# Batched matmul: the stores of batches 25 and 26 queued behind the last load instead of between the loads of batches 29 to 31

## The chip, the core and the metric

The kernel runs on one core of one Trainium2 chip. The metric is device microseconds (us) of one execution. Most executions of one kernel agree within 0.3%; a change counts as faster or slower from 2% on, with a 95% interval. A ratio of two kernels is the mean time of the fast runs of one over the mean of the fast runs of the other in the same rounds, so it isn't quite the ratio of the medians quoted beside it. A run is called fast if it isn't over 1.5% above the fastest one of its kernel.

Names used throughout: x29 is the load of x for batch 29, w29 that of its weight, s25 the store of batch 25's result. The last three batches' stores are named by half where they are issued by half (s31 first half, s31 second half). The "software queue" is the DMA queue that GpSimd (POOL) issues to; it carries all loads but the first x, and they are turned from float32 into bfloat16 on the way. The "hardware queue" is the one that SyncE (SP) issues to. Both run on the same 16 DMA engines.

## The reference

```python
batch, m, k, n = 32, 512, 1024, 768
x      = randn(batch, m, k)   # float32
weight = randn(batch, k, n)   # float32
out    = np.matmul(x, weight) # float32, 32 x 512 x 768
```

The kernel has to read 167.8 MB (67.1 of x, 100.7 of weights) and write 50.3 MB. Nothing is used twice, so no traffic can be saved.

## The kernel before

Each batch loads x and its weight as bfloat16, transposes x on the tensor engine, multiplies into PSUM (the tensor engine's result memory), copies the result to SBUF, the on-chip memory ("evacuation" below), and stores it. This is the part that the change touches (cuts are marked with `# ...`):

```python
CHUNKED = {B - 4: (4, 4), B - 3: (4, 4), B - 2: (4, 4), B - 1: (4, 2, 2)}
AHEAD = 3
LATE = 4
# ... pools: w has 4 buffers, x 5, out 7

def load_x(b):
    xs[b] = x_pool.tile([P, MT, K], BF16, name="x_sb")
    nc.gpsimd.dma_start(out=xs[b], in_=x_view[b])

def load_w(b):
    ws[b] = w_pool.tile([P, KT, N], BF16, name="w_sb")
    at = 0
    for n in CHUNKED.get(b, (KT,)):     # the last weights come in two or three pieces
        nc.gpsimd.dma_start(out=ws[b][:, at:at + n, :], in_=w_view[b, :, at:at + n, :])
        at += n

# ... first loads
for b in range(B):
    if b + AHEAD + 1 < B:
        load_x(b + AHEAD + 1)
    if b + AHEAD < B:
        load_w(b + AHEAD)
    if 0 < b <= B - LATE:               # stores 0 to 27: software queue
        nc.gpsimd.dma_start(out=out_view[b - 1], in_=outs[b - 1])
    if b == B - 1:                      # stores 28 to 30: hardware queue
        halves = [slice(pair * N2, (pair + 1) * N2) for pair in range(2)]
        nc.sync.dma_start(out_view[b - 1, :, halves[0]], outs[b - 1][:, halves[0]])
        for late in range(B - LATE, B - 2):
            nc.sync.dma_start(out_view[late], outs[late])
        nc.sync.dma_start(out_view[b - 1, :, halves[1]], outs[b - 1][:, halves[1]])
    outs[b] = out_pool.tile([P, MT * N], F32, name="out_sb")
    # ... transposes, matmuls, evacuation; batch 31 stores each half on the
    #     hardware queue as soon as it is evacuated
```

The order in the software queue at the end is thus: x29 w28 s24 x30 w29 s25 x31 w30 s26 w31 s27.

Of the kernel before, what the change touches and what calls it, by code (L numbers as in the profile page):

```python
# [12 lines left out]
@with_exitstack  # L13
def kernel(
    ctx: ExitStack,
    tc: tile.TileContext,
    x: bass.AP,
    weight: bass.AP,
    out: bass.AP,
):  # L20
    nc = tc.nc
    B, M, K = x.shape
    _, _, N = weight.shape
    P = 128
    MT = M // P
    KT = K // P
    JT = KT // 2
    N2 = 2 * N
    CHUNKED = {B - 4: (4, 4), B - 3: (4, 4), B - 2: (4, 4), B - 1: (4, 2, 2)}
    AHEAD = 3  # L30
    LATE = 4

    const = ctx.enter_context(tc.tile_pool(name="const", bufs=1))
    first_pool = ctx.enter_context(tc.tile_pool(name="first", bufs=1))
    w_pool = ctx.enter_context(tc.tile_pool(name="w", bufs=4))
    x_pool = ctx.enter_context(tc.tile_pool(name="x", bufs=5))
    xT_pool = ctx.enter_context(tc.tile_pool(name="xT", bufs=8))
    out_pool = ctx.enter_context(tc.tile_pool(name="out", bufs=7))
    tpsum = ctx.enter_context(tc.tile_pool(name="tpsum", bufs=2, space=bass.MemoryType.PSUM))
    mpsum = ctx.enter_context(tc.tile_pool(name="mpsum", bufs=2, space=bass.MemoryType.PSUM))  # L40



    w_view = weight.rearrange("b (ki ko) n -> b ki ko n", ki=P)
    x_view = x.rearrange("b (mi mo) k -> b mi mo k", mi=P)
    out_view = out.rearrange("b (mi mo) n -> b mi (mo n)", mi=P)

    xs, ws, outs = {}, {}, {}

    def banks():  # L50
        return [mpsum.tile([P, 512], F32, name=f"pm{i}") for i in range(3)]
# [8 lines that stand above are left out]
        for n in CHUNKED.get(b, (KT,)):  # L60
            nc.gpsimd.dma_start(out=ws[b][:, at:at + n, :], in_=w_view[b, :, at:at + n, :])  # L61
            at += n

    def transpose(b, mt):

        pt = tpsum.tile([P, JT, P], F32, name="pt")
        pairs = xs[b].bitcast(F32)
        for j in range(JT):
            nc.tensor.transpose(pt[:, j, :], pairs[:, mt, j::JT], ident)  # L69
        xT = xT_pool.tile([P, JT, P, 2], BF16, name="xT")  # L70
        nc.vector.tensor_copy(  # L71
            xT.rearrange("p j m r -> p (j m r)"), pt.bitcast(BF16).rearrange("p j m -> p (j m)")
        )
        return xT

    def transpose_first(mt):

        xT = xT_pool.tile([P, JT, P, 2], BF16, name="xT")
        for h in range(2):
            pt = tpsum.tile([P, JT, P], F32, name="pt")  # L80
            for i in range(JT):
                nc.tensor.transpose(pt[:, i, :], x_first[:, mt, JT * h + i::KT], ident)  # L82
            nc.vector.tensor_copy(  # L83
                xT[:, 2 * h:2 * h + 2].rearrange("p j m r -> p j r m"),
                pt.rearrange("p (j r) m -> p j r m", r=2),
            )
        return xT



    SPLITS = (
        ((0, 0, 0, 512), (1, 0, 512, N - 512)),
        ((1, N - 512, 0, 1024 - N), (2, 0, 1024 - N, N2 - 1024)),
    )

    def matmuls(pm, half, xT, b, kos, together):
        for ko in kos:
            for i, (bank, at, off, size) in enumerate(SPLITS[half]):
                shares = half == 1 and i == 0
                nc.tensor.matmul(  # L100
                    pm[bank][:, at:at + size],
                    xT[:, ko // 2, :, ko % 2],
                    ws[b][:, ko, off:off + size],
                    start=(ko == 0 and not (together and shares)),
                    stop=(ko == KT - 1),
                    skip_group_check=together,
                )

    def evacuate(b, pair, pm):
        o = outs[b][:, pair * N2:(pair + 1) * N2]  # L110
        nc.scalar.copy(o[:, 0:512], pm[0])  # L111
        nc.vector.tensor_copy(o[:, 512:1024], pm[1])  # L112
        nc.scalar.copy(o[:, 1024:N2], pm[2])  # L113

    with tc.manual_schedule():
        x_first = first_pool.tile([P, MT, K], F32)
        nc.sync.dma_start(x_first, x_view[0])
        load_w(0)
        ident = const.tile([P, P], F32)
        make_identity(nc, ident)  # L120
        for b in range(1, AHEAD):
            load_x(b)
            load_w(b)
        load_x(AHEAD)

        for b in range(B):
            if b + AHEAD + 1 < B:
                load_x(b + AHEAD + 1)
            if b + AHEAD < B:
                load_w(b + AHEAD)  # L130
            if 0 < b <= B - LATE:
                nc.gpsimd.dma_start(out=out_view[b - 1], in_=outs[b - 1])  # L132
            if b == B - 1:
                halves = [slice(pair * N2, (pair + 1) * N2) for pair in range(2)]
                nc.sync.dma_start(out_view[b - 1, :, halves[0]], outs[b - 1][:, halves[0]])
# [4 lines that stand above are left out]
            if b not in CHUNKED:  # L140
                turn = transpose if b else lambda _, mt: transpose_first(mt)
                xT = {mt: turn(b, mt) for mt in (0, 1)}
                for pair in range(2):
                    pm = banks()
                    for half in range(2):
                        if pair == 0:
                            matmuls(pm, half, xT[half], b, range(KT), False)
                            xT[2 + half] = turn(b, 2 + half)
                        else:
                            matmuls(pm, half, xT[2 + half], b, range(KT), False)  # L150
                    evacuate(b, pair, pm)
                continue
            xT = {0: transpose(b, 0)}
            pms = [banks() for _ in range(2)]
            at = 0
            for n in CHUNKED[b]:
                last = at + n == KT
                for mt in range(MT):
                    if mt + 1 not in xT and mt + 1 < MT:
                        xT[mt + 1] = transpose(b, mt + 1)  # L160
                    matmuls(pms[mt // 2], mt % 2, xT[mt], b, range(at, at + n), True)
                    if last and mt % 2 == 1:
                        pair = mt // 2
                        evacuate(b, pair, pms[pair])
                        if b == B - 1:
                            nc.sync.dma_start(out_view[b, :, halves[pair]], outs[b][:, halves[pair]])
                at += n
# [30 lines left out]
```

## Time and profile before

| what | value |
|---|---|
| time, median of 3 runs | 517.46 us (517.2 to 518.03) |
| span of the profiled execution | 515.2 us |
| DMA engines busy, 38 of the 40 slices | 90% or more |
| tensor engine busy | 83% |
| HBM traffic over the span | 423 GB/s |

First the page of the profile. The digit rows give the busy share of each of 40 equal slices in tenths (9 is 90% or more). GB/s counts a casting load at its two-byte side, so a slice of pure loads shows about 215 and one of pure stores about 425, for the same load on the engines. The last line is the chain of work that ended last, by engine.

```profile
span 515.2 us, 5979 instructions
...
PE   0999898798788888788887899787998787999793
...
DMA  8999999999999999999999999999999999999996
GB/s 254 219 215 213 218 274 273 254 239 277 276 275 270 234 270 276 273 274 244 253 278 274 275 256 241 275 276 275 266 243 263 275 279 269 247 251 274 274 384 275
...
DMA 88%; PE 8%; issue 1%; POOL 1%; DVE 0%; ACT 0%; POOLq 0%
```

DMA is full almost from end to end, and the chain is 88% DMA. How the queue is paced is seen in GpSimd's timeline of the kernel before: start, duration, line and operation, and in brackets the idle time before and what ended it.

```profile
373.09 0.53 POOL L55 DMA_DIRECT2D x_sb<-in_x_dram  x1 [6.66 <-DMA w_sb<-in_weight_dram]
376.75 0.53 POOL L61 DMA_DIRECT2D w_sb<-in_weight_dram  x1 [3.13 <-DMA out_dram<-out_sb]
381.68 0.54 POOL L132 DMA_DIRECT2D out_dram<-out_sb  x1 [4.40 <-DMA x_sb<-in_x_dram]
388.90 0.53 POOL L55 DMA_DIRECT2D x_sb<-in_x_dram  x1 [6.68 <-DMA w_sb<-in_weight_dram]
```

Each issue waits for an earlier transfer to land: an x issue for a weight, a weight's for a store, a store's for an x. That is the transfer eight places earlier, so about eight are always under way (the page's median from issue to landing is 39.6 to 43.2 us for whole transfers, some eight of them). The gaps are therefore the durations of transfers: 7.2 us for a weight (3.15 MB read), 3.66 for a store (1.57 MB), 4.9 for x (2.1 MB), 15.8 us a batch, at some 430 GB/s. 32 times 15.8 is 506 of the 515.2 us.

The end of the kernel, in two views of the kernel before. First the busy time of each engine in stretches of the end, with the granted clock (the share of its full clock that the tensor engine was given), the mean DMA share of 16 engines and GB/s in the last columns:

```profile
core 0: us, PE busy (x) PEld busy (x) DVE busy (x) ACT busy (x) POOL busy (x), PEclk, DMA share, GB/s
480.00:492.00 12.00, 11.15 (x61) 7.04 (x62) 2.07 (x3) 1.15 (x2) 0.00 (x0) 0.86 1.03 285
492.00:504.00 12.00, 11.70 (x77) 7.85 (x75) 3.36 (x5) 1.19 (x3) 0.00 (x0) 1.00 1.02 413
504.00:508.00 4.00, 2.78 (x17) 1.46 (x15) 1.38 (x2) 2.29 (x4) 0.00 (x0) 1.00 0.82 346
508.00:511.00 3.00, 0.00 (x0) 0.00 (x0) 0.00 (x0) 0.00 (x0) 0.00 (x0) 0.73 0.96 395
511.00:515.00 4.00, 0.00 (x0) 0.00 (x0) 0.00 (x0) 0.00 (x0) 0.00 (x0) 0.50 0.16 66
```

Then three lines of its timelines: the first matmuls of batch 30, the last of batch 31, and the issue of batch 31's two stores.

```profile
480.85 1.55 PE L100 MATMUL pm<-w_sb,xT 128*128 128x512 bf16 x8 [3.38 <-DMA w_sb<-in_weight_dram]
...
498.81 7.96 PE L100 MATMUL pm<-w_sb,xT 128*128 128x512 bf16 x48
...
506.12 1.63 SPq L166 DMA_DIRECT2D out_dram<-out_sb  x2
```

The tensor engine waits 3.38 us for w30 and works almost without a break from then to 506.8 us. DMA share drops to 0.82 just there, between 504 and 508 us; batch 31's stores are issued only from 506.12 us on.

### The profile page before, as it was taken

The numbers are of one execution on the slowest core, as the hardware profiler recorded it, in microseconds if no ns is written. First come the engines' busy times: TensorE is split into PE (matmuls) and PEld (weight loads), VectorE is DVE, ScalarE is ACT, GpSimd is POOL, SyncE is SP. The second block draws the span as 40 slices with busy tenths as digits, with TensorE's granted clock in tenths as the row PEclk, the third lists the DMA queues.
The fourth block names the chain that finished last, engine by engine and source line by source line (L and its number), as shares of the span: only waits on it lengthen the run. The fifth ranks groups of instructions, "written<-read, shape, count | busy, mean of one in ns | idle before, by whom it ended". The sixth has DMA issues, their size and how long they took to land.

```text
span 515.2 us, 5979 instructions
## 1 busy us (share of the span) xinstructions
PE 429.3 (83%) x2576; PEld 279.5 (54%) x2576; DVE 129.8 (25%) x196; ACT 76.2 (15%) x129; POOL 51.7 (10%) x102
## 2 busy tenths in 40 slices
PE   0999898798788888788887899787998787999793
PEld 0666465465455555455554556454665455665461
DVE  0433232313223313133132232222331223232231
ACT  0011111111011111111111111010111111111011
POOL 3010100011001010100101001100101010111000
PEclk9999899989889989799898999898999889899897
DMA  8999999999999999999999999999999999999996
GB/s 254 219 215 213 218 274 273 254 239 277 276 275 270 234 270 276 273 274 244 253 278 274 275 256 241 275 276 275 266 243 263 275 279 269 247 251 274 274 384 275
DMA packets 14857, 135.64 MB, mean 263 GB/s; under 512 B 1648, under 2 KB 1648, under 8 KB 3312
## 3 DMA queue, kind: packets, MB, share of 16 engines
q0 software_dynamic: 13824, 126.88, 96.8%
q1 hardware_dynamic: 1008, 8.39, 4.0%
q8 instruction: 20, 0.33, 0.2%
q14 instruction: 5, 0.04, 0.0%
HBM read 167.77 MB, written 50.33 MB: 423 GB/s over the span
## 4 chain that ended last, share of the span: by engine, by line
DMA 88%; PE 8%; issue 1%; POOL 1%; DVE 0%; ACT 0%; POOLq 0%
DMA w_sb<-in_weight_dram 40%; DMA out_dram<-out_sb 25%; DMA x_sb<-in_x_dram 23%; PE pm L100 7%; PE pt L69 1%; POOL w_sb L61 0%; POOL x_sb L55 0%; DVE out_sb L112 0%; DVE xT L71 0%; ACT out_sb L113 0%; POOL ident masks.py:199 0%; POOL ident masks.py:197 0%; POOLq L132 0%; POOLq L61 0%; POOLq masks.py:199 0%
## 5 line engine op out<-in xcount | busy, mean ns | idle before, releaser
L100 PE MATMUL pm<-w_sb,xT 128*128 128x256 bf16 (+1 forms) x2048 | 374.5, 342 | 65.2 <-DMA w_sb<-in_weight_dram 63.7
L100 PEld LDWEIGHTS <-xT 128*128 128x128 bf16 x2048 | 207.5, 102 | 207.7 <-issue 72.5
L71 DVE COPY xT<-pt 128x1024 bf16<-128x1024 bf16 x124 | 82.8, 689 | 230.0 <-PE pt L69 230.0
L111 ACT COPY out_sb<-pm 128x512 f32<-128x512 f32 x64 | 37.5, 585 | 293.2 <-PE pm L100 293.2
L112 DVE COPY out_sb<-pm 128x512 f32<-128x512 f32 x64 | 43.9, 687 | 128.1 <-PE pm L100 128.1
L69 PEld LDWEIGHTS pt<-ident,x_sb 128*128 128x128 f32 x496 | 72.6, 207 | 6.3 <-issue 1.0
L69 PE MATMUL pt<-ident,x_sb 128*128 128x128 f32 x496 | 75.1, 285 | 0.0
L113 ACT COPY out_sb<-pm 128x512 f32<-128x512 f32 x64 | 37.5, 586 | 137.3 <-PE pm L100 137.2
L55 POOL DMA_DIRECT2D x_sb<-in_x_dram x31 | 16.4, 532 | 176.8 <-DMA w_sb<-in_weight_dram 151.3
L61 POOL DMA_DIRECT2D w_sb<-in_weight_dram x37 | 19.7, 534 | 126.3 <-DMA out_dram<-out_sb 59.7
L132 POOL DMA_DIRECT2D out_dram<-out_sb x28 | 15.0, 537 | 118.1 <-DMA x_sb<-in_x_dram 56.4
L82 PE MATMUL pt<-ident,x_first 128*128 128x128 f32 x32 | 6.0, 351 | 12.3 <-DMA x_first<-in_x_dram 12.3
L82 PEld LDWEIGHTS pt<-ident,x_first 128*128 128x128 f32 x32 | 5.0, 204 | 12.9 <-issue 12.2
L83 DVE CAST xT<-pt 128x512 bf16<-128x512 f32 x8 | 5.6, 726 | 19.4 <-PE pt L82 19.1
L111 ACT ACT_TABLE_LOAD x1 | 1.3, 1283 | 0.7 <-PEq L182 0.7
masks.py:199 POOL TENSOR_SCALAR_AFFINE_SELECT ident<-ident 128x128 f32<-128x128 f32 x1 | 0.3, 287 | 0.1
masks.py:197 POOL MEMSET ident<- 128x128 f32 x1 | 0.2, 223 | 0.0
L182 POOL MEMSET const-float32-0.0<- 128x1 f32 x1 | 0.1, 98 | 0.2 <-issue 0.2
L182 POOL MEMSET const-bfloat16-1.0<- 128x1 bf16 x1 | 0.1, 101 | 0.0
L182 POOL MEMSET const-uint8-127<- 128x1 uint8 x1 | 0.1, 101 | 0.0
L182 POOL MEMSET const-float32-1.0<- 128x1 f32 x1 | 0.1, 98 | 0.0
## 6 DMA issues: line engine op xcount, KB each, us to landing
w_sb<-in_weight_dram POOLq DMA_DIRECT2D x28, 1536.0 KB, 43.2
out_dram<-out_sb POOLq DMA_DIRECT2D x28, 1536.0 KB, 42.0
x_sb<-in_x_dram POOLq DMA_DIRECT2D x31, 1024.0 KB, 39.6
w_sb<-in_weight_dram POOLq DMA_DIRECT2D x7, 768.0 KB, 31.4
out_dram<-out_sb SPq DMA_DIRECT2D x4, 768.0 KB, 7.6
out_dram<-out_sb SPq DMA_DIRECT2D x2, 1536.0 KB, 13.7
x_first<-in_x_dram SPq DMA_DIRECT2D x1, 2048.0 KB, 11.4
w_sb<-in_weight_dram POOLq DMA_DIRECT2D x2, 384.0 KB, 27.5
```

The lines of the kernel that those rows point to most:

```text
L55: nc.gpsimd.dma_start(out=xs[b], in_=x_view[b])
L61: nc.gpsimd.dma_start(out=ws[b][:, at:at + n, :], in_=w_view[b, :, at:at + n, :])
L69: nc.tensor.transpose(pt[:, j, :], pairs[:, mt, j::JT], ident)
L71: nc.vector.tensor_copy(xT.rearrange("p j m r -> p (j m r)"), pt.bitcast(BF16).rearrange("p j m -> p (j m)"))
L82: nc.tensor.transpose(pt[:, i, :], x_first[:, mt, JT * h + i::KT], ident)
L83: nc.vector.tensor_copy(xT[:, 2 * h:2 * h + 2].rearrange("p j m r -> p j r m"), pt.rearrange("p (j r) m -> p j r m", r=2),)
L100: nc.tensor.matmul(pm[bank][:, at:at + size], xT[:, ko // 2, :, ko % 2], ws[b][:, ko, off:off + size], start=(ko == 0 and not (together an ...
L111: nc.scalar.copy(o[:, 0:512], pm[0])
L112: nc.vector.tensor_copy(o[:, 512:1024], pm[1])
L113: nc.scalar.copy(o[:, 1024:N2], pm[2])
L132: nc.gpsimd.dma_start(out=out_view[b - 1], in_=outs[b - 1])
L182: nc = _bacc.Bacc("TRN2", target_bir_lowering=False, num_devices=1)
```

## The change

Its intent: the last loads should not stand behind stores that nobody waits for, so that the tensor engine gets its last operands earlier.

```diff
+    HELD = 3
...
+        pending = []
         for b in range(B):
             if b + AHEAD + 1 < B:
                 load_x(b + AHEAD + 1)
             if b + AHEAD < B:
                 load_w(b + AHEAD)
-            if 0 < b <= B - LATE:
-                nc.gpsimd.dma_start(out=out_view[b - 1], in_=outs[b - 1])
+            if b <= B - LATE:
+                if b > 0:
+                    pending.append(b - 1)
+                if b + AHEAD < B - HELD or b == B - LATE:
+                    for at in pending:
+                        nc.gpsimd.dma_start(out=out_view[at], in_=outs[at])
+                    pending = []
```

The order in the software queue becomes: x29 w28 s24 x30 w29 x31 w30 w31 s25 s26 s27. No transfer, byte or instruction is added or removed.

## The prediction

> **What bounds the kernel now.** The DMA engines, nearly from first microsecond to last. The page's slices show DMA at 9 tenths or more in 38 of 40; the chain that ended last is 88% DMA, 8% PE. In GpSimd's timeline a batch between 341 and 408 us takes 15.8 us, a sum of transfers: 7.2 us for a weight (3.15 MB read), 3.66 for a store (1.57 MB), 4.92 for x (2.1 MB), all near 430 GB/s. 32 times 15.8 is 506 of the span's 515.2 us. PE is 83% busy and waits 63.7 us for weights (view of waits). Each software-queue issue waits for the landing of the one eight before it (x_sb issues release on a weight, weights on a store, stores on an x_sb).
>
> **What the change does.** It adds and removes no transfer, byte or instruction. The queue's end goes from x29 w28 s24 x30 w29 s25 x31 w30 s26 w31 s27 to x29 w28 s24 x30 w29 x31 w30 w31 s25 s26 s27. x31 and w30 are ahead by one store (3.66 us), w31 by two (7.3 us). With seven output buffers no evacuation waits for the held stores. Several transfers stay queued at each issue, so nothing starves.
>
> Before, w30's first half landed at 480.7 us and PE had idled 3.4 us for it; w31 landed 491.7 to 495.4, before PE missed it. After, w30 should land near 477.0, w31 between 484.4 and 488.1. Batch 29 ends near 477.6, so batch 30 follows almost without a gap; batch 31 should end near 503 instead of 507.4.
>
> **How much lies on the critical path: almost none.** What ends the kernel is the drain of stores. DMA share falls to 0.82 in 504 to 508 us (windows), which looks like 0.75 us of waiting for batch 31's stores. But that is a mean of 16 engines. The Trainium skill ("DMA: Bandwidth & Descriptors", section "Why a DMA increments its semaphore by 16 and not by 1") says that each engine posts its own +1. The trace records these increments; for one store they spread over 4.6 us. The slowest engine's, for the last stores, come at 504.60, 508.25, 510.13, 511.95 and 513.79 us: 3.65 us per whole store, 1.82 to 1.88 per half, the full rate, without a hole. Only the fast engines idled. Issuing the last stores 4 us earlier lengthens the slowest one's queue and doesn't shorten its work.
>
> A small cost: two queues carry stores together for longer. Before, store 27 with half a store took 5.54 us (495.41 to 500.95) for 2.36 MB, 426 GB/s against 430: over some 9 MB about 0.2 us. I estimate a gain of 0 to 0.8 us and a cost of 0 to 0.3.
>
> **Predicted: 517.3 us** (before 517.46), range 516.2 to 518.3; faster by over 2%: 0.01, within 2%: 0.98, slower by over 2%: 0.01.
>
> **What would show each step.** Right: w30 lands near 477 and PE's wait for it falls from 3.4 us to under 1; PE's last matmul ends near 503; yet the last store's increment stays within 0.7 us of 513.8. DMA share stays near 1.0 through 508. Wrong: PE's end doesn't move (the stores hadn't delayed the loads), or the last increment comes earlier as PE does (the stores' issue was on the path), or over 1 us later (a long pure-store phase is slower than the mix).
>
> **What would make it wrong.** A different rate when both queues only write; the spread of the engines, which grew from 3.55 to 4.6 us after 420 us and may fall otherwise in another run (about 1 us either way).

## The result, and the profile after

| | before | after |
|---|---|---|
| median | 517.15 us (516.99 to 518.03, 6 runs) | 517.17 us (517.0 to 519.47, 6 runs) |
| ratio of fast runs | | 1.0003, 95% interval 0.9987 to 1.002 |

The same time. The profiled execution of the changed kernel was by chance its longest one (519.47 us, span 517.7; the five others took 517.0 to 517.53). These are lines of its page: the span, DMA, GB/s and the chain by engine.

```profile
span 517.7 us, 5931 instructions
...
DMA  8999999999999999999999999999999999999995
GB/s 254 218 217 213 216 273 274 263 230 275 277 273 276 240 257 276 274 278 257 242 272 275 276 270 241 262 275 271 265 243 251 277 275 263 252 242 214 305 425 245
...
DMA 75%; PE 20%; DVE 1%; issue 1%; another core or an unknown queue 1%; ACT 0%; POOLq 0%
```

Since such a run is no fair partner, the unaltered changed kernel was run and profiled once more (run after_again, below: 516.95 us, span 515.1; a single run, so its state is put down as unknown, but its time lies with the fast runs). The comparison uses that trace. Its windows, with the same columns as before:

```profile
480.00:492.00 12.00, 11.80 (x77) 7.95 (x76) 3.35 (x5) 2.35 (x4) 0.00 (x0) 1.00 1.04 344
492.00:504.00 12.00, 11.42 (x70) 7.22 (x72) 3.27 (x6) 2.00 (x4) 0.00 (x0) 1.00 1.01 425
504.00:508.00 4.00, 0.00 (x0) 0.00 (x0) 0.20 (x1) 0.30 (x1) 0.00 (x0) 0.84 0.99 416
508.00:511.00 3.00, 0.00 (x0) 0.00 (x0) 0.00 (x0) 0.00 (x0) 0.00 (x0) 0.50 0.72 301
511.00:515.00 4.00, 0.00 (x0) 0.00 (x0) 0.00 (x0) 0.00 (x0) 0.00 (x0) 0.50 0.15 61
```

And the same three places of its timelines (the line numbers have moved):

```profile
479.37 1.48 PE L101 MATMUL pm<-w_sb,xT 128*128 128x512 bf16 x8 [0.30 <-DVE xT L72]
...
495.72 7.96 PE L101 MATMUL pm<-w_sb,xT 128*128 128x512 bf16 x47
...
503.03 1.63 SPq L173 DMA_DIRECT2D out_dram<-out_sb  x2
```

All that the change aimed at has happened. The tensor engine no longer waits for w30 (0.30 us for a copy of VectorE in place of 3.38 us for a weight). Its last matmul ends at 503.7 us instead of 506.8, the last stores are issued 3.1 us earlier, and the dip of 504 to 508 us is filled: 0.99 in place of 0.82. Yet the span is 515.1 against 515.2 us. What was gained at 504 to 508 us is missing at 508 to 511, where the share is now 0.72 in place of 0.96.

The reason lies below that mean of 16 engines. Each of this kernel's 103 transfers has sixteen increments of its semaphore in the trace (1,648 in all), one for each engine. For the last transfers these are the times of the first and of the last of the sixteen increments, in us (worked out from the records of the trace, rounded to 0.01):

```
            before               after_again
            first    last        first    last
w29 end     463.91  468.54       463.83  468.51     <- same queue up to here
w30 part 1  476.07  480.71       472.35  477.04
w31 end     490.78  495.41       483.39  488.07
s28         499.98  504.60       499.89  504.59
s29         503.64  508.25       503.55  508.23
s30 half 2  505.47  510.13       505.40  510.08
s31 half 1  509.20  511.95       507.24  511.93
s31 half 2  511.09  513.79       509.09  513.77
```

The loads come 3.7 and 7.3 us earlier, as intended. But the column of the slowest engine ends at the same time. (The records name no engine. That the last increment is each time that of the same engine is read from the lag, which is 4.61 to 4.67 us for each of s28, s29 and s30 half 2 before.) In the kernel before, its increments for s28, s29 and the halves follow each other after 3.65, 1.88, 1.82 and 1.84 us: full speed, no hole. It never waited for batch 31's stores, since it was still busy with the earlier ones. Only the fast engines waited (their increment for s31's second half came at 511.09 us), and only they have gained: 2.0 us. The slowest one has gained 0.02 us, and the kernel ends with it.

### The profile page after: what moved, and what is told of

It is laid out like the page before. It is cut to its first block, busy times and chain, and to the rows that moved or that the text cites. A ratio compares the mean times of both kernels' runs of the same rounds, so it can differ in the third digit from the quotient of the medians.

```text
span 517.7 us, 5931 instructions
## 1 busy us (share of the span) xinstructions
PE 423.7 (82%) x2528; PEld 278.5 (54%) x2576; DVE 129.9 (25%) x196; ACT 76.2 (15%) x129; POOL 51.7 (10%) x102
## 2 busy tenths in 40 slices
DMA packets 14857, 135.64 MB, mean 262 GB/s; under 512 B 1648, under 2 KB 1648, under 8 KB 3312
## 4 chain that ended last, share of the span: by engine, by line
DMA 75%; PE 20%; DVE 1%; issue 1%; another core or an unknown queue 1%; ACT 0%; POOLq 0%
DMA w_sb<-in_weight_dram 32%; DMA out_dram<-out_sb 25%; PE pm L101 17%; DMA x_sb<-in_x_dram 16%; DMA x_first<-in_x_dram 2%; PE pt L70 2%; PE pt L83 1%; DVE xT L72 1%; DVE out_sb L113 1%; ACT out_sb L114 0%; POOLq L138 0%; POOLq L62 0%; POOLq L56 0%
## 5 line engine op out<-in xcount | busy, mean ns | idle before, releaser
L101 PE MATMUL pm<-w_sb,xT 128*128 128x256 bf16 (+1 forms) x2000 | 369.0, 339 | 68.6 <-DMA w_sb<-in_weight_dram 63.0
```

What stands on the lines that cost most here:

```text
L101: nc.tensor.matmul(pm[bank][:, at:at + size], xT[:, ko // 2, :, ko % 2], ws[b][:, ko, off:off + size], start=(ko == 0 and not (together an ...
```

## The experiments

"Idle matmuls" below are 20 or 40 matmuls of 512 columns at the start of batch 31, whose result the real ones overwrite; they lengthen the tensor engine's work without touching a transfer.

```diff
             at = 0
+            if b == B - 1:
+                for _ in range(20):        # or 40
+                    nc.tensor.matmul(pms[0][0][:, 0:512], xT[0][:, 0, :, 0],
+                                     ws[b][:, 0, 0:512], start=True, stop=True, skip_group_check=True)
             for n in CHUNKED[b]:
```

All the differences below are under 2%, so by the rule above each kernel is "the same"; they are read from the ratios and their intervals.

**Theory:** the slowest DMA engine is busy from start to end, so the time is the sum of its transfers; the tensor engine has slack, which the change widens. **Rivals:** the end follows the tensor engine, and a gain there is eaten by a slower phase of pure stores; or the dip in the DMA share is on the path.

### 1 to 4: how much slack the tensor engine has

> The kernel before, with 20 idle matmuls of 512 columns (about 0.23 us each, 4.6 us together, overwritten afterwards, so the result stays right) at the start of batch 31. My theory (the slowest DMA engine is busy to the end; the tensor engine has slack of about 2.7 us before the last store, worked out from the trace: an unhindered last half store lands 3.1 us after its issue plus its predecessor's 0.5, that is at 511.05, and it landed at 513.79): +1.9 us. Rival 1 (the end follows batch 31's last evacuation): +4.6 us. Rival 2 (nothing before the drain matters at all): 0.

> The same 20 idle matmuls in the changed kernel. My theory: the change has moved the tensor engine's end ahead by some 4.5 us and so widened its slack from 2.7 to about 7 us: 0 against the kernel before, within 0.5. Rival 1 (end follows the last evacuation, and the change's gain of 4.5 us there is eaten by a slower store phase): +4.6 us like the other one.

> 40 idle matmuls, 9.2 us, in the kernel before. My theory: +6.5 us (9.2 less the slack of 2.7). Rival 1: +9.2. Rival 2: 0.

> 40 idle matmuls, 9.2 us, in the changed kernel. My theory: +2 us (9.2 less a slack of 7), thus 4.5 us less than the kernel before with the same burden: the reordering does take 4.5 us from the tensor engine's chain, which is worth nothing until that chain is made the longer one. Rival 1: +9.2.

All four ran with 11 runs of the kernel before (median 517.04 us). All results were right.

| idle matmuls | in the kernel before | in the changed kernel |
|---|---|---|
| 20 | 519.5 us, ratio 1.0042 (1.003 to 1.0054) | 517.13 us, ratio 1.0 (0.9988 to 1.0012) |
| 40 | 522.92 us, ratio 1.0106 (1.0092 to 1.0121) | 518.94 us, ratio 1.004 (1.0028 to 1.0052) |

In us (517.1 times the ratio less one): +2.2 and +5.5 before, 0 and +2.1 after. The expected values were +1.9, +6.5, 0 and +2. Rival 1 had foreseen 4.6 and 9.2 in all of them, rival 2 nothing in the kernel before. The issue of batch 31's stores in the four traces (in the order before with 20 and 40, after with 20 and 40):

```profile
511.22 1.63 SPq L172 DMA_DIRECT2D out_dram<-out_sb  x2
```

```profile
517.58 1.63 SPq L172 DMA_DIRECT2D out_dram<-out_sb  x2
```

```profile
506.37 1.63 SPq L179 DMA_DIRECT2D out_dram<-out_sb  x2
```

```profile
510.64 1.63 SPq L179 DMA_DIRECT2D out_dram<-out_sb  x2
```

An estimate from the trace of before: its fast engines finished s31 at 511.09 us with an issue at 506.12, which is 4.97 us for both halves. By that rule the four would end no earlier than 516.19, 522.55, 511.34 and 515.61 us. Their last increments came at 516.35, 522.72, 514.01 and 515.78. The first, second and fourth are set by the late issue, within 0.2 us. The third is set by the slowest engine's other work, 0.2 us from the 513.8 of both plain kernels. So the issue becomes the limit only if it comes later than about 508.8 us (513.8 less 5.0). The kernel before issues at 506.12 and has 2.7 us of slack; the changed one issues at 503.03 in its trace and has 5.8 there.

That 5.8 us is low for the changed kernel. In its trace the granted clock was 0.79 and 0.64 between 464 and 470 us, and batch 30's matmuls began only at 479.37 us. In the traces with 20 and 40 idle matmuls the clock was 1.00 there, and they began at 477.93 and 477.88 us. The 40 idle matmuls delayed the real ones by 9.1 us and cost 2.1, which leaves a slack of about 7 us, as was expected; by the issue times of these two traces it is 7.2 to 7.3.

One size was off: +5.5 us with 40 idle matmuls before, where +6.5 was expected. In the trace of before the tensor engine ran for 4 us (482 to 486) at a granted clock of 0.52 and 0.62; runs without such a stretch would have more slack. That is argued, not shown: the traces with idle matmuls in the old order have such a stretch too (0.56 and 0.59 with 20; 0.50 and 0.74, 2 us later, with 40). The profiled run of this kernel was its longest, 525.85 us, because w30 came 2.3 us late there, so it isn't used for the size.

### 5 and 6: one store taken away

```diff
-            if 0 < b <= B - LATE:
+            if 0 < b <= B - LATE and b - 1 != 25:
```

(in the changed kernel: `if at == 25: continue` in the loop over `pending`)

> The kernel before without the store of batch 25 (result wrong in that batch on purpose). My theory (time is the sum of the transfers on the slowest engine): -3.65 us, one store. Rival (the order of the loads sets the end): about the same here, since loads move ahead too.

> The changed kernel without the store of batch 25, which stands behind all loads there (result wrong in that batch on purpose). My theory: -3.65 us against the kernel before, as much as in the other order. Rival (the loads and the tensor engine behind them set the end): 0, since no load moves.

The results are wrong in batch 25. Measured beside 517.36 us (7 runs): 513.77 us, ratio 0.9927 (0.9907 to 0.9947), in the kernel before, and 513.8 us, ratio 0.9926 (0.9904 to 0.9947), in the changed one. A store's 3.65 us is a ratio of 0.9929. Taking 1.57 MB away is worth its transfer time wherever it stands in the queue; moving it is worth nothing.

### 7: less work for the tensor engine at the end

```diff
         for ko in kos:
+            if b == B - 1 and ko in (4, 5):
+                continue
```

> The kernel before with a quarter of batch 31's matmuls left out (result wrong in that batch on purpose), so the tensor engine ends about 2.7 us earlier and no transfer changes. My theory: 0, within 0.5. Rival (the DMA idle time of 504 to 508 us is on the path): -0.75 us; rival (end follows the last evacuation): -2.7.

The result is wrong in batch 31. 517.2 us beside 517.36, ratio 0.9991 (0.9973 to 1.0009). The stores were issued at 503.61 us instead of 506.12, and the last increment came at 513.94. This does to the tensor engine's end nearly what the change does, without the change, and it is worth as little.

### 8: five stores held back instead of three

```diff
-    HELD = 3
+    HELD = 5
```

> The changed kernel with stores 23 to 27 held back instead of 25 to 27: the loads move ahead by up to two more stores, the pure store phase grows from 7 to 9 stores. My theory: 0, within 0.5, since no byte changes. Rival (a gain from earlier loads and a cost of a longer pure store phase cancel in the change): they need not cancel twice, so some -0.5 or +0.5 us or more.

Right result, 517.4 us beside 517.36, ratio 0.9994 (0.9976 to 1.0012). Batch 31's stores were issued at 500.57 us, 5.5 us earlier than in the kernel before; the last increment came at 514.21. So the phase of pure stores can be made longer still without gain or loss. A gain and a cost that cancel by chance, in the change and here again, are unlikely after this.

### 9: the changed kernel once more

> The changed kernel once more, unaltered, because its profiled execution was the longest of its runs (519.47 us against 517.0 to 517.5): my theory expects a span of 515.2 to 515.9 us, the slowest engine's increment for batch 31's second half near 514, and the last matmul near 502.5, 4 us before that of the kernel before.

516.95 us, span 515.1, the slowest engine's last increment at 513.77, the last matmul at 503.7 (1.2 us later than expected). This is the trace shown above.

It also says where the 2.5 us of the first profiled run (span 517.7) came from. There the slowest engine's increment for the end of w29 came at 471.06 us, against 468.51 here and 468.54 in the kernel before. Up to that transfer the queues of all three are the same. So the loss was there before the change could act. Of it, 1.2 us is a wider spread (one engine was 5.8 us behind the first, not 4.6), the other 1.3 us met all engines; why is open.

### 10 to 12: what makes engines slow

The spread between the sixteen engines is 0.6 us at the first load and 4.6 us at the end of the kernel before. In the kernel before, one engine's lag behind the first jumps from 3.5 to 4.6 us between the landings at 423.6 and 429.6 us, and another's between those at 445.4 and 449.6. At 423.88 and 447.55 us the trace has 16 KB packets on the queue that the profile calls "instruction". There are 20 of them, each lasting 0.89 to 0.98 us on one engine. The Trainium skill ("Runtime: NRT & Kernel Launch", section "Instruction fetch mechanics") says that instructions come in blocks of 16 KiB, 256 instructions, through a DMA queue of the sequencer's own. If each one delays the engine that carries it, more instructions should cost time, and fewer save some.

> The kernel before with each matmul of 512 columns made into two of 256: 1,024 more matmuls and as many weight loads for the same result, no transfer of data changed. Both traces show 20 instruction fetches of 16 KB, each on one engine for about 0.93 us, and after each the landing of one engine is about 1.1 us later for good. If fetches make the slow engines slow: some 8 more fetches, about 28, the spread of landings grows from 4.6 to 5.5 us or more, and the time by 1 to 2 us. Rival (the spread has another cause): spread and time as before, within 0.5 us, unless the tensor engine becomes the limit, which its busy share would show.

```diff
-        ((0, 0, 0, 512), (1, 0, 512, N - 512)),
-        ((1, N - 512, 0, 1024 - N), (2, 0, 1024 - N, N2 - 1024)),
+        ((0, 0, 0, 256), (0, 256, 256, 256), (1, 0, 512, N - 512)),
+        ((1, N - 512, 0, 1024 - N), (2, 0, 1024 - N, 256), (2, 256, 1280 - N, 256)),
```

(with the start flag on the first piece of a PSUM bank only)

> The kernel before with half of all its matmuls left out in every batch (four of eight contraction steps; result wrong on purpose), so 1,024 matmuls and as many weight loads fewer and the tensor engine about half as busy; no data transfer is changed. The run with more instructions had 28 fetches of 16 KB instead of 20, a spread of 5.85 us instead of 4.65, and took 1.4 us longer. My theory (the fetches make the slow engines slow, and the slowest engine sets the time): 12 fetches, spread about 2.5 to 3.5 us, time 1 to 2 us below the kernel before. Rival (the tensor engine's chain counts at the end): some 6 us less, as batch 31's matmuls shrink by half. Rival (neither counts): 0.

```diff
         for ko in kos:
+            if ko in (2, 3, 4, 5):
+                continue
```

The instruction queue in the three kernels: the one with halved matmuls, the one before, the one with split matmuls (packets, MB, share of 16 engines).

```profile
q8 instruction: 12, 0.20, 0.1%
```

```profile
q8 instruction: 20, 0.33, 0.2%
```

```profile
q8 instruction: 28, 0.46, 0.3%
```

| kernel | fetches | spread near the end | time | ratio |
|---|---|---|---|---|
| half the matmuls (wrong result) | 12 | 3.7 us | 516.32 us | 0.9986 (0.9972 to 0.9999) |
| before | 20 | 4.6 us | 517.0 to 517.16 us | 1 |
| matmuls split in two (right result) | 28 | 5.8 us | 518.53 us | 1.0027 (1.0013 to 1.004) |

The number of fetches moved by eight each time, as 2,048 instructions in blocks of 256 would have it. The time follows them in both directions: +1.4 us and -0.7 us. The spread is one trace's value each, and it is not set by the number of fetches alone: in ten other traces with 20 fetches it lay between 4.6 and 5.8 us before the last stores (5.8 in the first profiled run of the changed kernel), so 5.8 with 28 isn't outside that range, while 3.7 with 12 is. What else differs between runs stays open; that the spread is how more fetches cost time is argued from the jumps, not shown. In the run with split matmuls the slowest engine's last increments came at 511.42, 513.26 and 515.10 us, again without a hole, so the tensor engine isn't what made it longer. Halving the tensor engine's work gave 0.7 us, at the low end of what the interval can tell from nothing and less than the 1 to 2 expected; the rival with the tensor engine at the end would have given some 6.

> The changed kernel, with rows 96 to 127 of stores 28 and 29 sent as four transfers of 8 rows each. If a transfer of 8 rows runs on eight engines, the first eight, these get 10 rows of each store and the other eight 6 instead of 8: 24.6 KB less per store, about 0.9 us at an engine's rate of 27 GB/s, 1.8 us for both. If the slow engines are the last eight: the spread falls from 4.6 to about 2.8 us and the time by about 1.8 us. If the first eight: the spread and the time grow by about 1.8 us. If the slow ones are mixed, or the small transfers run on all engines: no fall.

```diff
-                    nc.sync.dma_start(out_view[late], outs[late])
+                    nc.sync.dma_start(out_view[late, 0:96], outs[late][0:96])
+                    for p in range(96, P, 8):
+                        nc.sync.dma_start(out_view[late, p:p + 8], outs[late][p:p + 8])
```

This was an attempt to move bytes from slow engines to fast ones, and it failed: 520.83 us, ratio 1.0064 (1.0051 to 1.0078), right result. Two lines of SyncE's timeline show why it can't be read as a test of balance:

```profile
491.06 16.24 SPq L146 DMA_DIRECT2D out_dram<-out_sb  x4
...
510.17 3.02 SPq L175 DMA_DIRECT2D out_dram<-out_sb  x2
```

The hardware queue too lets an issue wait for the transfer eight places earlier, so the small transfers held SyncE for 16 us (the last three were issued at 499.12, 504.58 and 507.03 us, each within 0.02 us of the landing of such an earlier one), and batch 31's stores were issued at 510 us or later. By the rule of experiments 1 to 4 that alone costs over a microsecond. The profiled run was again the longest of its kernel (524.65 us; the others 519.95 to 521.3), with its last increment at 521.4 us; what beyond the late issue made it so late is open. One thing can be read: the first small transfer had one record right after its issue and eight more, spread over 7.4 us. It ran on eight engines, as a rule of the Trainium skill gives for 8 rows ("DMA: Bandwidth & Descriptors", section "Why a DMA increments its semaphore by 16 and not by 1"), and both fast and slow ones seem to be among them. Which engines fetch instructions stays open, because the records name no engine. No version was found that beats both kernels.

## Why the prediction was right

- **"What bounds the kernel now. The DMA engines"**: shown. One store less is worth its 3.65 us in either order (runs 5 and 6), and the tensor engine's end can move by 5.5 us towards the start without effect (runs 7 and 8).
- **"x31 and w30 are ahead by one store, w31 by two"**: shown. w30's first part landed at 477.04 us (predicted near 477.0), w31 from 484.36 to 488.07 (predicted 484.4 to 488.1).
- **"Batch 31 should end near 503 instead of 507.4"**: right in kind, smaller in size in the trace shown. The last matmul ended at 503.7 instead of 506.8 us, 3.1 us earlier and not 4.4. Batch 29 ended at about 479 us, not at 477.6, so batch 30 began at 479.37. Most of the difference is the stretch of lower granted clock between 464 and 470 us; in the changed kernel with idle matmuls, without that stretch, batch 30 began at 477.9.
- **"Only the fast engines idled"**: shown. The fastest engine's last increment came 2.0 us earlier, the slowest's 0.02 us. The mean DMA share, taken alone, would have promised 0.75 us. The Trainium skill ("Perfetto Trace Analysis", section "What "DMA-bound" means") lists specific DMA engines as one of the things that a DMA-bound kernel can be bound on; this is such a case.
- **"A small cost ... about 0.2 us"**: not seen. From the end of w29 to the last increment the slowest engine took 45.25 us before and 45.26 after, so gain and cost are both zero within this reading.
- **"The spread of the engines ... may fall otherwise in another run (about 1 us either way)"**: it did, in the first profiled run of the changed kernel. That run was 2.5 us longer, 1.2 of it from the spread. The stated size was too small for that one run, not for the median.

The slack is what the change really buys: 2.7 us before, 5.8 after in the trace shown, and about 7 by the runs with idle matmuls. It is worth nothing until something makes the tensor engine's end later, and then up to 3.4 us (522.6 or so against 519.2 with 40 idle matmuls: 517.1 times 1.0106 and 1.004).

## What to carry to other kernels

Before you move work forward at the end of a DMA-bound kernel, ask whether the slowest DMA engine has a hole there. Look at the last of the sixteen increments of each transfer, not at the mean share: a dip in the mean can be fast engines resting. Here the slowest one had no hole: a store less was worth 3.65 us, and a better order merely added slack to the other engines. In such a kernel even the number of instructions can count: eight more fetches went with 1.4 us here.

## What the Trainium skill lacked or had wrong

- "Runtime: NRT & Kernel Launch", section "Instruction fetch mechanics": it calls the cost of crossing a 16 KiB boundary mostly hidden. It doesn't say that in a DMA-bound kernel a fetch takes the time of an engine that the data need. Here each of 20 fetches occupied one DMA engine for 0.89 to 0.98 us, and two that were followed left an engine about 1.1 us further behind. 12, 20 and 28 fetches went with times of 516.3, 517.1 and 518.5 us, so eight fetches went with 0.7 to 1.4 us, 0.1 to 0.3% of the time.
- "DMA: Bandwidth & Descriptors", section "Latency and other measured facts": it names engines 7 and 15 as the usual slow ones, and descriptor rings as a best guess. Here four of 16 engines were over 4 us behind the first at the end, and the spread grew through the run, in the two steps that were followed after instruction fetches. Which engines these were, the trace doesn't tell, so it neither confirms nor refutes the page.
- No page gives a test for whether a dip in the mean DMA share costs anything. Here the last of the sixteen increments gave one: the share was 0.82 in 504 to 508 us before and 0.99 after, with the last increment at 513.79 and 513.77 us.
